# The last half of the output columns computed in PSUM behind the last gather, the final work on one engine, and an account with exact extents

## The chip, the cores and the metric

The kernel runs on one core of one Trainium2 chip. The metric is the device time of one execution in microseconds (us), measured from a launch on the chip; the profile's span, from the first to the last instruction, is somewhat shorter. TensorE (PE) multiplies into PSUM banks, VectorE (DVE), ScalarE (ACT) and GpSimd (POOL) work on SBUF (and DVE and ACT on PSUM), SyncE (SP) issues most of the DMAs, POOL some. Each engine works through its own instructions in program order.

## The reference

One layer of a streaming encoder, for 2048 tokens of 1024 channels behind 16 learned meta tokens, in float32:

```python
u = rms_norm(h, pre_g)
proj = u @ w_in                       # 7 x 512 columns
# glu_a, glu_b, conv_gate, q, k, v, sb_gate
c = causal_depthwise_conv(glu_a * sigmoid(glu_b), conv_w, conv_b)   # width 31
c = (silu(layer_norm(c)) @ w_pw2 + b_pw2) * silu(conv_gate)
s = stick_breaking_attention(heads(q), heads(k), heads(v))          # 8 heads x 64
s = s * silu(sb_gate)
mixed = concatenate([c, s], axis=-1) @ w_out
return h + rms_norm(mixed, post_g)
```

The attention is strictly causal: the weight of a key is sigmoid(z) times the product of 1 - sigmoid(z) over the keys between it and the query. Since the final normalisation needs the sum of squares over all 1024 output columns of a token, nothing of a token's output can leave before all its columns are there.

## The kernel before

The tokens are worked on in four chunks of 512 (TC). All large products are made at float32 accuracy from a rounded high part and the rest as a low part, three matmuls for one (hi x hi, hi x lo, lo x hi). A weight slab arrives raw (`wr<-wpack`, 512 KB, a ring of two), ACT rounds its high half (`w<-wr`), POOL takes the difference (`w<-wr,w`); both halves are saved in DRAM by POOL (`wscr<-w`) and read back in later chunks (`w<-wscr`, ring of four, at the end also `wr<-wscr`). `load_raw` issues the raw loads, `prepare` fills the rings, `weights` hands a slab to a product and `release` frees it. In `attention` each step is one product q x k (`T<-kk,q`), a sigmoid on ACT (`T<-T`), a scan on DVE (`pr<-T,pr`), four transposes on PE (`T<-ident,pr`), the high and low part of the result on ACT (`ah<-T`) and DVE (`al<-T,ah`), and the products with the values (`av<-ah,vk`, `av<-al,vk`), called gather. Eight heads of 64 channels go in four pairs; a pair's result, gated, becomes one of four `mixs` slabs of 128 rows, the convolution's result the four `mixc` slabs.

The order is made when the kernel is built, by a list scheduler: `merge` takes pieces of the attention as its main stream and pieces of projections and of the output product as filling between them, in shares that the table `SHARES` gives for each chunk. It chooses by an account, the `Clock`: every instruction that is issued adds an estimated time to its engine, and `Clock.at` tells when a tile will be ready. Work that isn't due yet waits as `Later` in the list `soon`, and `step`, `force` and `run` issue it. So a change of an estimate or of a rule moves instructions everywhere; what was issued first stands first in its engine's queue.

In the last chunk, `last_room` reuses two large tiles for what the end needs, `later_part` loads the last 128 rows of w_out early (`ev<-wpack` four times, split on ACT and POOL into `acc` tiles) and calls `out_part`. That makes the output product for the first seven of eight 128-row slabs (k below 7) of the mixer's result, in four column groups of 256 (OC); each group for two halves of 256 tokens. Three groups go by ACT into the SBUF tiles `y`; the last group stays in two `mm` banks, and the end of its second half (`keep["rest"]`) is made in `out_last`, when the heads are done. When the last head's gather has been made, `finish_late` computes the last `mixs` slab, and `out_last` works through four blocks of 128 tokens (`add_up`): the products of the last slab (`T<-acc,mixs`, `mm<-acc,mixs`), additions to `y` on DVE, squares summed on ACT, multiplication by post_g on POOL for the first 512 columns and on DVE for the rest, then `rate` (the reciprocal root by a power on POOL) and `give_out` (scaling, addition of x, and the DMA of the output; of the first two blocks the second half by ACT and POOL, all the rest by DVE).

## Time and profile before

| | before |
|---|---|
| median of 3 runs | 1373.24 us (1370.44 to 1373.45) |
| the profiled execution | 1371.76 us, span 1370.0 us |
| PE busy | 1312.5 us, 96% of the span |
| DVE busy | 1006.8 us, 73% |
| ACT busy | 732.0 us, 53% |
| POOL busy | 657.0 us, 48% |
| moved by DMA | 299.12 MB, mean 218 GB/s |
| mean granted TensorE clock | 0.992 |

The engines work side by side, so their shares don't add up. The profile names an instruction by its engine, its operation and the tiles out<-in; numbers behind a tile's name are left out. All instructions are recorded at one helper's line, so one goes by tiles and not by lines. Idle time of an engine is given with what ended it: "[4.83 <-DVE al]" says that the engine stood for 4.83 us until DVE had written `al`.

### The profile page before, as it was taken

To read this page: it belongs to the slowest core of one execution; us is meant where nothing else is said; L and a number is where in the kernel's file an instruction comes from. 1 tells how busy PE (TensorE), PEld (TensorE's weight loads), DVE (VectorE), ACT (ScalarE), POOL (GpSimd) and SP (SyncE) were. 2 spreads that over 40 slices of the span, in tenths; PEclk is the share of its full clock that TensorE was granted. 3 is DMA by queue.
4 is the path that set the end of the run, shared out by engine and by line. 5 is a ranking of instruction groups with operands and counts; after the bars stand their busy time and mean duration, and the time that the engine had idled before them with its cause. 6 is when DMAs were issued, how large, how long until landed. Compare 5 with 4: busy or idle time off the path is not lost. (4 is left out here: it accounts for less than half of the span.)

```text
span 1370.0 us, 21785 instructions
## 1 busy us (share of the span) xinstructions
PE 1312.5 (96%) x7599; PEld 1125.2 (82%) x7599; DVE 1006.8 (73%) x1402; ACT 732.0 (53%) x1452; POOL 657.0 (48%) x794
## 2 busy tenths in 40 slices
PE   6999988999998999999999999999999999999895
PEld 5998877887788977887789988888777898888794
DVE  3999663998984467984495477885549988898666
ACT  5233554444446544476655456578676576655443
POOL 5445486668356631387831243278786111222303
PEclk9999999999999999999999999999999999999998
DMA  4266978999975994686866696567677456587431
GB/s 142 94 164 197 345 233 248 302 316 320 348 245 179 319 339 145 202 236 204 264 223 185 191 326 198 173 190 235 201 220 241 147 173 174 173 276 237 159 109 62
DMA packets 160157, 299.12 MB, mean 218 GB/s; under 512 B 15392, under 2 KB 69344, under 8 KB 160048
## 3 DMA queue, kind: packets, MB, share of 16 engines
q1 hardware_dynamic: 145744, 247.65, 58.9%
q0 software_dynamic: 14304, 50.08, 9.4%
q8 instruction: 60, 0.98, 0.3%
q14 instruction: 49, 0.40, 0.1%
HBM read 216.02 MB, written 81.66 MB: 217 GB/s over the span
## 5 line engine op out<-in xcount | busy, mean ns | idle before, releaser
L204 PE MATMUL mm<-uh,w 128*128 128x512 f32 (+1 forms) x1728 | 522.9, 367 | 2.6 <-POOL w L204 1.5
L204 PEld LDWEIGHTS mm<-uh,w 128*128 128x128 f32 x1728 | 307.6, 188 | 51.5 <-POOL w L204 2.5
L204 DVE TENSOR_TENSOR al<-T,ah 128x512 fp32r<-128x512 f32 (+3 forms) x323 | 194.4, 602 | 168.9 <-ACT ah L204 167.9
L204 PE MATMUL mm<-ul,w 128*128 128x512 f32 (+1 forms) x864 | 312.0, 361 | 0.0
L204 DVE TENSOR_TENSOR_SCAN pr<-T,pr,zcol 128x512 f32<-128x512 f32 x192 | 245.1, 1277 | 55.5 <-ACT T L204 51.4
L204 ACT ACTIVATE ah<-T 128x512 fp32r<-128x512 f32 (+3 forms) x323 | 171.7, 532 | 164.7 <-PE T L204 159.5
L204 DVE SCALAR_TENSOR_TENSOR cv<-ct,cp,cv 128x512 f32<-128x512 f32 x319 | 239.4, 751 | 7.5
L204 ACT ACTIVATE T<-T 128x512 f32<-128x512 f32 (+2 forms) x320 | 167.6, 525 | 96.6 <-PE T L204 92.7
L204 POOL TENSOR_TENSOR acc<-acc,pd 128x512 f32<-128x512 f32 x150 | 193.8, 1292 | 50.6 <-ACT pd L204 43.7
L204 PE MATMUL T<-kk,q 128*128 128x512 f32 (+2 forms) x640 | 195.3, 388 | 2.9 <-DVE pr L204 1.7
L204 POOL TENSOR_TENSOR w<-wr,w 128x512 fp32r<-128x512 f32 x116 | 149.7, 1296 | 98.5 <-ACT w L204 95.2
L204 PE MATMUL T<-ident,pr 128*128 128x128 f32 x1088 | 173.2, 275 | 9.8 <-DVE al L204 6.5
L204 PEld LDWEIGHTS mm<-ul,w 128*128 128x128 f32 x864 | 162.7, 188 | 20.3 <-DVE ul L204 0.2
L204 PEld LDWEIGHTS T<-ident,pr 128*128 128x128 f32 x1088 | 134.1, 141 | 42.3 <-DVE al L204 8.2
L204 DVE TENSOR_TENSOR_SCAN pr<-T,tri 128x128 f32<-128x128 f32 (+3 forms) x128 | 103.8, 815 | 43.0 <-ACT T L204 42.5
L204 ACT ACTIVATE w<-wr 128x512 fp32r<-128x512 f32 x116 | 72.3, 628 | 104.8 <-DMA wr<-wpack 34.9
L204 PEld LDWEIGHTS T<-kk,q 128*128 128x128 f32 x640 | 106.1, 190 | 19.1 <-DVE pr L204 2.8
L204 PE MATMUL av<-ah,vk 128*128 128x512 f32 (+1 forms) x320 | 117.0, 366 | 1.4 <-ACT ev L204 1.4
L204 PE MATMUL av<-al,vk 128*128 128x512 f32 (+1 forms) x320 | 117.4, 367 | 0.0
L204 PE MATMUL mm<-uh,wr 128*128 128x512 f32 x320 | 115.0, 401 | 0.0
L204 ACT ACTIVATE pd<-ct,cp 128x512 f32<-128x512 f32 x150 | 105.9, 717 | 15.3 <-POOL acc L204 14.7
L204 POOL COPY cm<-pr 128x1 f32<-128x1 f32 x120 | 23.3, 206 | 153.4 <-DVE pr L204 153.2
(154 smaller groups left out, 1768.3 us busy)
## 6 DMA issues: line engine op xcount, KB each, us to landing
w<-wscr SPq DMA_DIRECT2D x125, 512.0 KB, 4.2
wscr<-w POOLq DMA_DIRECT2D x76, 512.0 KB, 5.8
wr<-wscr SPq DMA_DIRECT2D x59, 512.0 KB, 4.3
wr<-wpack SPq DMA_DIRECT2D x58, 512.0 KB, 5.2
kk<-kscr SPq DMA_DIRECT2D x80, 256.0 KB, 5.2
vk<-vscr SPq DMA_DIRECT2D x80, 256.0 KB, 4.1
q<-qscr SPq DMA_DIRECT2D x64, 256.0 KB, 6.8
tok<-x SPq DMA_DIRECT2D x16, 512.0 KB, 7.6
```

The costliest lines, as they stand in the source:

```text
L204: return call(out, *args, **kw)
```

## The change

*Tail.* `out_part` takes only the first two column groups into `y`. For the last two, `late(0, ...)` makes the product of k below 7 for tokens 0 to 255 in the banks `cv` and `mm` during the attention; `late(1, ...)` for tokens 256 to 511, in the banks `mm` and `T`, becomes `keep["rest"]`, so that it stands in `out_last`, with three steps ahead of the first final products and the others behind them. The weights of these groups are loaded a second time for it. In `out_last` DVE does all multiplications, additions and scalings; POOL keeps four powers and one memset; the addition of epsilon becomes a fourth column of the sums. `AHEAD` goes, and one corner of `SHARES` for the last chunk moves from 136.0 to 126.3.

*Account.* `Clock.at` looks at the parts of a tile that were written with their full extent instead of their offset; `Later` pieces get an order in which nested ones stand with their parent, and only earlier ones are forced by a later instruction. A new rule in `merge` (`early`) runs a waiting piece whose time has come before the next attention step; `load_raw` loads one raw slab at a time as such a piece; `room_for_turned` keeps transposes from being issued when the ring of `ah` has no free tile.

*Late split.* The split of the last 128 rows of w_out is put into `soon` with a date 6 and 7 us ahead.

```diff
-AHEAD = 2
-    [(29.8, 172.7)], [(73.1, 217.8)], [(116.0, 217.8)], [(125.1, 97.4), (160.4, 136.0)],
+    [(29.8, 172.7)], [(73.1, 217.8)], [(116.0, 217.8)], [(125.1, 97.4), (160.4, 126.3)],
...
         lo, hi = extent(ap)
-        hit = [t for o, t in parts.items() if lo <= o <= hi]
-        return max(hit or parts.values())
+        return max([0.0] + [t for (a, b), t in parts.items() if a <= hi and lo <= b])
...
-        self.n = Later.count
+        self.n = (*clock.here, Later.count)
...
             for a in (*ins, *outs):
-                for e in c.writers(a):
+                for e in c.writers(a, c.here):
                     self.run(e)
...
+            if c + 1 < NCH:
+                yield from proj_specs(c + 1)
+            else:
+                for n in (*range(0, D, OC), *range(D // 2, D, OC)):
+                    yield w_out, n, OC, 0, KD - 1
...
-    def load_raw():
-        while todo_raw and len(raws) < RAWS:
+    def load_raw(most=RAWS):
+        while todo_raw and len(raws) < most:
...
-                    in_us(2.0, load_raw)
+                    when(
+                        lambda: load_raw(min(RAWS, len(raws) + 1)), [], date=pe.now + 2.0, tag="wr")
...
-                    yield need(*f[0]["a"], tag="T")
+                    yield need(*f[0]["a"], tag="T", given=room_for_turned)
...
-        for n in range(0, D, OC):
+        for n in range(0, D // 2, OC):
...
+        def late(i, tags):
+            for e in range(2):
+                w = weights(w_out, D // 2 + e * OC, OC, 0, KD - 1)
+                keep["o", i, e] = yield from out_products(
+                    w, mix, range(KD - 1), i, False, tag=tags[e], free=True
+                )
+
+        yield from late(0, ("cv", "mm"))
+        keep["rest"] = late(1, ("mm", "T"))
...
+        def add_first(tb, a):
+            yt = y[tb // 2][:, tb % 2, 0:TC]
+            dve.tensor_tensor(yt, yt, a, op=ALU.add)
+            square(tb, yt, 0)
+            dve.tensor_tensor(yt, yt, pg[:, 0], op=ALU.mult)
+
+        def add_second(tb):
+            yt = y[tb // 2][:, tb % 2, TC:]
+            for e in range(2):
+                o, cols = keep["o", tb // 2, e][:, tb % 2], slice(e * OC, (e + 1) * OC)
+                square(tb, o, 1 + e)
+                dve.tensor_tensor(yt[:, cols], o, pg[:, 1, cols], op=ALU.mult)
...
-            dve.tensor_scalar(ss, ss, 1e-6, None, op0=ALU.add)
...
-                if h and tb < 2:
-                    act.activation(yt[:, cols], yt[:, cols], AF.Copy, scale=r)
-                    pool.tensor_tensor(xr, xr, yt[:, cols], op=ALU.add)
-                else:
-                    dve.scalar_tensor_tensor(xr, yt[:, cols], r, xr, op0=ALU.mult, op1=ALU.add)
+                dve.scalar_tensor_tensor(
+                    xr, y[tb // 2][:, tb % 2, cols], rates[tb], xr, op0=ALU.mult, op1=ALU.add
+                )
...
+        rest = keep["rest"]
+        for _ in range(3):
+            next(rest)
+        a = [first(0)]
+        second(0)
+        a += [first(tb) for tb in range(1, NTB)]
+        add_first(0, a[0])
+        finish_off(rest)
+        second(1)
+        add_second(0)
+        add_first(1, a[1])
+        rate(0)
+        add_second(1)
+        add_first(2, a[2])
+        rate(1)
+        give_out(0)
+        add_first(3, a[3])
+        give_out(1)
+        add_second(2)
+        rate(2)
+        add_second(3)
+        rate(3)
+        give_out(2)
+        give_out(3)
...
+            early = [e for e in soon if e.at() < s.at()] if s.at() > pe.now + LEAD else ()
+            if early:
+                run(min(early, key=lambda e: e.at()))
+                continue
             s.go()
...
-            split(raw, hi, lo)
+            in_us(
+                6.0 + i, lambda raw=raw, hi=hi, lo=lo: split(raw, hi, lo), [raw], [hi, lo]
+            )
```

The first place is the end of PE's queue, from the last gathers on (`av<-ah,vk` and `av<-al,vk`), before:

```order
L204 MATMUL av<-ah,vk 128x512
L204 MATMUL av<-al,vk 128x512
L204 MATMUL av<-ah,vk 128x512
L204 MATMUL av<-al,vk 128x512
L204 MATMUL mm<-w,mixs 128x256 x6
L204 MATMUL mm<-w,mixc 128x256 x24
L204 MATMUL mm<-w,mixs 128x256 x18
L204 MATMUL T<-acc,mixs 128x512 x3
L204 MATMUL T<-acc,mixs 128x256 x3
L204 MATMUL mm<-acc,mixs 128x256 x6
L204 MATMUL T<-acc,mixs 128x512 x3
L204 MATMUL T<-acc,mixs 128x256 x3
```

and of the change:

```order
L203 MATMUL av<-ah,vk 128x512
L203 MATMUL av<-al,vk 128x512
L203 MATMUL mm<-w,mixc 128x256 x12
L203 MATMUL mm<-w,mixs 128x256 x18
L203 MATMUL mm<-wr,mixc 128x256 x24
L203 MATMUL T<-acc,mixs 128x512 x3
L203 MATMUL cv<-acc,mixs 128x256 x6
L203 MATMUL mm<-acc,mixs 128x256 x6
L203 MATMUL T<-acc,mixs 128x512 x9
L203 MATMUL mm<-w,mixs 128x256 x18
L203 MATMUL T<-w,mixc 128x256 x24
L203 MATMUL T<-wr,mixs 128x256 x18
```

Behind the last gather stood 48 matmuls of 256 columns ahead of the first product of the last `mixs` slab (`T<-acc,mixs`); now there are 54, and 60 more (18, 24, 18) behind the final products of all four blocks' first half.

The second place is the end of DVE's queue, from the first addition of the third block on, before (`tok` are the tiles `y`, `uh` holds post_g, `ul` holds x):

```order
L204 TENSOR_TENSOR tok<-tok,T 128x512
L204 TENSOR_REDUCE ss<-sq_15301 128x1
L204 TENSOR_SCALAR ss<-ss 128x1
L204 TENSOR_TENSOR tok<-tok,T 128x256
L204 TENSOR_TENSOR tok<-mm,uh 128x256
L204 TENSOR_TENSOR tok<-tok,uh 128x256
L204 TENSOR_REDUCE ss<-sq_15331 128x1
L204 TENSOR_SCALAR ss<-ss 128x1
L204 SCALAR_TENSOR_TENSOR ul<-tok,st_15338,ul 128x512 x2
L204 SCALAR_TENSOR_TENSOR ul<-tok,st_15349,ul 128x512 x2
```

and of the change, from the first addition of the third block on:

```order
L203 TENSOR_TENSOR tok<-tok,T 128x512
L203 TENSOR_TENSOR tok<-tok,uh 128x512
L203 TENSOR_REDUCE ss<-sq_15155 128x1
L203 SCALAR_TENSOR_TENSOR ul<-tok,st_15302,ul 128x512 x2
L203 TENSOR_TENSOR tok<-tok,T 128x512
L203 TENSOR_TENSOR tok<-tok,uh 128x512
L203 SCALAR_TENSOR_TENSOR ul<-tok,st_15316,ul 128x512 x2
L203 TENSOR_TENSOR tok<-mm,uh 128x256
L203 TENSOR_TENSOR tok<-T,uh 128x256
L203 TENSOR_REDUCE ss<-sq_15155 128x1
L203 TENSOR_TENSOR tok<-mm,uh 128x256
L203 TENSOR_TENSOR tok<-T,uh 128x256
```

The four multiplications of 512 columns (`tok<-tok,uh`) are new on this engine, the additions of 256 columns and the addition of epsilon (`ss<-ss`) are gone, and the multiplications of 256 columns now read their product from a PSUM bank (`cv`, `mm`, `T`).

The third place is SP's queue between chunk 0 and chunk 1, where values for the next chunk's attention (`vm`, `vk`), gates (`gscr`) and raw weights (`wr`) are moved, before:

```order
L204 DMA q_1989<-qscr 64x2x512 x2
L204 DMA kk<-kscr 128x512
L204 DMA wr<-wpack 128x2x512
L204 DMA gscr<-ev 128x512
L204 DMA wr<-wpack 128x2x512
L204 DMA gscr<-ev 128x512
L204 DMA wr<-wpack 128x2x512
L204 DMA vm<-vscr 16x64 x16
L204 DMA vk<-vscr 128x4x128
L204 DMA q_2221<-qscr 64x2x512 x2
L204 DMA kk<-kscr 128x512
L204 DMA wr<-wpack 128x2x512 x4
```

and of the change:

```order
L203 DMA q_1988<-qscr 64x2x512 x2
L203 DMA kk<-kscr 128x512
L203 DMA gscr<-ev 128x512
L203 DMA wr<-wpack 128x2x512 x2
L203 DMA gscr<-ev 128x512
L203 DMA vm<-vscr 16x64 x16
L203 DMA vk<-vscr 128x4x128
L203 DMA wr<-wpack 128x2x512 x2
L203 DMA q_2270<-qscr 64x2x512 x2
L203 DMA kk<-kscr 128x512
L203 DMA wr<-wpack 128x2x512 x3
```

The write of `gscr` now stands ahead of the first of these raw loads, and the raw load that stood ahead of the 16 `vm` loads stands behind them and `vk`, with another one, ahead of `q`. On ACT, whose two roundings of a slab (`w<-wr`) stand near the normalised tokens of chunk 1 (`uh<-T,cp`), before:

```order
L204 ACTIVATE mixc<-mm 128x512
L204 ACTIVATE w<-wr 128x512 x2
L204 ACTIVATE T<-T 128x128
L204 ACTIVATE mixc<-mm 128x512
L204 ACTIVATE uh<-T,cp 128x512 x3
L204 ACTIVATE w<-wr 128x512 x2
L204 ACTIVATE ah<-T 128x128
L204 ACTIVATE T<-T 128x256
L204 ACTIVATE uh<-T,cp 128x512 x2
```

and of the change:

```order
L203 ACTIVATE mixc<-mm 128x512
L203 ACTIVATE w<-wr 128x512 x2
L203 ACTIVATE ah<-T 128x256
L203 ACTIVATE T<-T 128x128
L203 ACTIVATE mixc<-mm 128x512
L203 ACTIVATE w<-wr 128x512 x2
L203 ACTIVATE uh<-T,cp 128x512 x3
L203 ACTIVATE ah<-T 128x128
L203 ACTIVATE T<-T 128x256
L203 ACTIVATE uh<-T,cp 128x512 x2
```

The two roundings behind the first three `uh` stand ahead of them now.

## Rows read from the trace of the kernel before

**Rows 1.** The page: the span, and the busy time of each engine with its share of the span and its instructions.

```profile
span 1370.0 us, 21785 instructions
...
PE 1312.5 (96%) x7599; PEld 1125.2 (82%) x7599; DVE 1006.8 (73%) x1402; ACT 732.0 (53%) x1452; POOL 657.0 (48%) x794
```

**Rows 2.** Busy time of each engine in five stretches (columns: stretch in us and its length; busy us and instructions of PE, PEld, DVE, ACT and POOL; the granted TensorE clock; the share of DMA time; GB/s).

```profile
165.00:225.00 60.00, 51.12 (x250) 41.43 (x249) 30.78 (x40) 31.86 (x61) 38.24 (x48) 0.97 0.76 243
225.00:1265.00 1040.00, 1024.85 (x5711) 866.83 (x5709) 775.79 (x1053) 590.93 (x1168) 511.50 (x611) 1.00 0.73 234
...
1294.30:1328.00 33.70, 33.70 (x250) 31.66 (x249) 22.34 (x30) 15.41 (x30) 0.92 (x1) 1.00 0.43 129
1328.00:1342.10 14.10, 14.10 (x105) 13.07 (x105) 5.41 (x9) 4.79 (x8) 0.00 (x0) 1.00 0.15 49
...
1353.65:1370.00 16.35, 0.00 (x0) 0.00 (x0) 12.60 (x21) 3.99 (x14) 8.04 (x8) 0.61 0.34 128
```

**Rows 3.** Timeline of PE around the last attention product (columns: start, us, engine, line, operation, out<-in, shapes, count; in brackets the idle time before and what ended it). A line groups neighbours that follow each other.

```profile
1341.71 0.39 PE L204 MATMUL av<-al,vk 128*128 128x512 f32 x1
1341.93 0.88 PE L204 MATMUL mm<-w,mixs 128*128 128x256 f32 x6
...
1345.53 2.32 PE L204 MATMUL mm<-w,mixs 128*128 128x256 f32 x18
1347.68 1.21 PE L204 MATMUL T<-acc,mixs 128*128 128x512 f32 x6
```

**Rows 4.** Timeline of DVE over the tail, same columns.

```profile
1343.47 0.42 DVE L204 TENSOR_TENSOR uh<-uh 128x256 f32<-128x256 f32 x1
...
1348.58 1.02 DVE L204 TENSOR_TENSOR tok<-tok,T 128x512 f32<-128x512 f32 x2 [2.26 <-PE T L204]
...
1350.46 1.22 DVE L204 TENSOR_TENSOR tok<-tok,uh 128x256 f32<-128x256 f32 x1 [0.38 <-ACT ev L204]
...
1354.62 1.74 DVE L204 SCALAR_TENSOR_TENSOR ul<-tok,st,ul 128x512 f32<-128x512 f32 x1
...
1360.99 0.67 DVE L204 TENSOR_TENSOR tok<-tok,T 128x512 f32<-128x512 f32 x1
1361.59 0.14 DVE L204 TENSOR_REDUCE ss<-sq 128x1 f32<-128x3 f32 x1
...
1364.23 2.73 DVE L204 SCALAR_TENSOR_TENSOR ul<-tok,st,ul 128x512 f32<-128x512 f32 x4
```

**Rows 5.** Timeline of ACT over the tail: the squares of 512 and of 256 columns.

```profile
1349.30 0.63 ACT L204 ACTIVATE ev<-tok 128x512 bf16<-128x512 f32 x1 [3.44 <-DVE tok L204]
...
1350.33 0.36 ACT L204 ACTIVATE ev<-mm 128x256 bf16<-128x256 f32 x1
```

**Rows 6.** Timeline of POOL over the tail: one of its multiplications.

```profile
1353.15 1.26 POOL L204 TENSOR_TENSOR tok<-tok,uh 128x512 f32<-128x512 f32 x1
```

**Rows 7.** Timelines of ACT (two rows) and of PE (one row) at the start.

```profile
13.60 2.18 ACT L204 ACTIVATE w<-wr 128x512 fp32r<-128x512 f32 x4
15.68 1.83 ACT L204 ACTIVATE uh<-T,cp 128x512 fp32r<-128x512 f32 x3
...
17.19 2.41 PE L204 MATMUL T<-ident,tok 128*128 128x128 f32 x16 [0.99 <-DVE ul L204]
```

**Rows 8.** Timeline of SP (SPq is its queue) between chunk 0 and chunk 1: DMA issues, their time in the queue and their count.

```profile
176.45 0.39 SPq L204 DMA_DIRECT2D wr<-wpack  x1
176.94 0.52 SPq L204 DMA_DIRECT2D gscr<-ev  x1
...
191.76 0.38 SPq L204 DMA_DIRECT2D wr<-wpack  x1
192.20 9.88 SPq L204 DMA_DIRECT2D vm<-vscr  x16
...
205.06 10.91 SPq L204 DMA_DIRECT2D wr<-wpack  x3
```

**Rows 9.** Timelines of ACT (two rows) and of PE (three rows) between chunk 0 and chunk 1.

```profile
169.79 1.06 ACT L204 ACTIVATE ev<-tok 128x1024 bf16<-128x1024 f32 x1 [1.13 <-DMA gscr<-ev]
...
212.35 1.15 ACT L204 ACTIVATE w<-wr 128x512 fp32r<-128x512 f32 x2 [7.80 <-DMA wr<-wpack]
...
172.74 0.33 PE L204 MATMUL T<-ident,pr 128*128 128x128 f32 x1 [1.50 <-DVE pr L204]
174.01 0.47 PE L204 MATMUL mm<-uh,w 128*128 128x512 f32 x1 [0.95 <-DVE ev L204]
...
214.04 1.11 PE L204 MATMUL T<-ident,pr 128*128 128x128 f32 x4 [4.83 <-DVE al L204]
```

**Rows 10.** Busy time in the two stretches between 165 and 1290 us in which the granted clock was about half (columns as in rows 2).

```profile
213.60:217.05 3.45, 3.01 (x9) 2.57 (x10) 3.36 (x6) 3.04 (x7) 3.45 (x5) 0.51 0.12 15
1275.20:1282.00 6.80, 6.05 (x20) 4.73 (x20) 6.25 (x12) 1.93 (x6) 1.82 (x3) 0.50 0.26 78
```

**Rows 11.** Timelines of ACT (one row) and of PE (three rows) where the last raw weights arrive.

```profile
1271.34 0.63 ACT L204 ACTIVATE acc<-ev 128x512 fp32r<-128x512 f32 x1 [2.90 <-DMA ev<-wpack]
...
1273.24 0.66 PE L204 MATMUL T<-ident,pr 128*128 128x128 f32 x4 [1.26 <-DVE al L204]
1274.43 0.51 PE L204 MATMUL T<-kk,q 128*128 128x256 f32 x2 [0.53 <-DVE pr L204]
...
1276.25 1.65 PE L204 MATMUL T<-ehl,vm 128*128 128x512 f32 x3 [0.75 <-DVE al L204]
```

More of the change, by code (lines that the diff above doesn't have):

```diff
@@ L91, in __init__, with readers @@
         self.soon = []
+        self.here = ()
     def writers(self, ap, before=None):
         return [e for e in self.soon if e.touches(e.outs, ap) and (not before or e.n < before)]
-    def readers(self, ap):
-        return [e for e in self.soon if e.touches(e.ins, ap)]
+    def readers(self, ap, before=None):
+        return [e for e in self.soon if e.touches(e.ins, ap) and (not before or e.n < before)]
     def at(self, ap, before=None):
@@ L180, in issue @@
             for a in (*ins, *outs):
-                for e in c.writers(a):
+                for e in c.writers(a, c.here):
                     self.run(e)
             for a in outs:
-                for e in c.readers(a):
+                for e in c.readers(a, c.here):
                     self.run(e)
@@ L200, in issue @@
             for a in outs:
-                c.ready.setdefault(a.name, {})[a.offset] = done
+                c.ready.setdefault(a.name, {})[extent(a)] = done
             for a in (*outs, *near):
@@ L261, in run @@
             soon.remove(e)
+            here, clock.here = clock.here, e.n
             e.what()
+            clock.here = here
     def force(mark):
-        for e in clock.writers(mark):
-            run(e)
+        while clock.writers(mark):
+            run(clock.writers(mark)[0])
     def when(what, ins, outs=(), engine=None, date=0.0, tag=None):
@@ L393, in step, with tap @@
             tap_apart()
-    def tap():
-        if next(taps[0], None) is None:
-            taps.popleft()
+    def tap(some=taps):
+        here, clock.here = clock.here, ()
+        if next(some[0], None) is None:
+            some.popleft()
+        clock.here = here
     def tap_apart():
-        if next(taps_apart[0], None) is None:
-            taps_apart.popleft()
+        tap(taps_apart)
     def fill_gap(when):
@@ L477, in chunk @@
                 yield w_pw2, j * P, P, 0, NJ
-            yield from proj_specs(c + 1) if c + 1 < NCH else out_specs(0, KD - 1)
+            if c + 1 < NCH:
[3 more added lines that the diff above has]
+                    yield w_out, n, OC, 0, KD - 1
         for spec in proj_specs(0):
@@ L1018, in load_first, with room_for_turned @@
             keep["first", c] = load_q(c, 0), load_k(0, c)
+    def room_for_turned():
+        return clock.oldest("ah", 3) not in hold
     def attention(c, mixs):
@@ L1290, in meta_keys @@
             fetch(js[0])
-        yield need(bm, tag="T")
+        yield need(bm, tag="T", given=None if part else room_for_turned)
         hold.remove(bm.name)
@@ L1321, in meta_keys, with out_products @@
             mixs[j] = hi, lo
-    def out_products(w, mix, ks, half, whole=True, bank=None, there=None):
+        hold.remove(ah.name)
+    def out_products(w, mix, ks, half, whole=True, bank=None, there=None, tag="mm", free=None):
         fresh = bank is None
@@ L1333, in out_products @@
                 nxt = [m for kk in pair for m in mix(kk)]
-                yield need(wh, wl, *nxt, tag=None if bank is not None else "mm")
+                yield need(wh, wl, *nxt, tag=None if bank is not None else tag)
             if bank is None:
-                bank = PT("mm", [P, 2, OC])
+                bank = PT(tag, [P, 2, OC])
             for b in range(2):
@@ L1345, in out_products @@
                 pe.matmul(o, ml, wh, start=False, stop=(whole and i == len(ks) - 1 and b == 1))
-            if half and (k % 2 or i == len(ks) - 1):
+            if (half if free is None else free) and (k % 2 or i == len(ks) - 1):
                 release()
@@ L1355, in out_part @@
         there = lambda k: k < NJ or k - NJ in mixs[c]
-        for n in range(0, D, OC):
-            last = n == D - OC
+        for n in range(0, D // 2, OC):
             w = weights(w_out, n, OC, 0, KD - 1)
@@ L1367, in out_part @@
             for i in range(2):
-                part = out_products(w, mix, ks, i, not last, banks[i], there)
-                if last and i == 1:
-                    first = next(part)
-                    for _ in range(AHEAD):
-                        yield first
-                        first = next(part)
-                    keep["rest"] = part
-                    return
-                b = yield from part
-                if last:
-                    keep["o", 0] = b
-                else:
-                    act.activation(y[i][:, :, n : n + OC], b, AF.Copy)
+                b = yield from out_products(w, mix, ks, i, True, banks[i], there)
+                act.activation(y[i][:, :, n : n + OC], b, AF.Copy)
+        def late(i, tags):
[6 more added lines that the diff above has]
+        keep["rest"] = late(1, ("mm", "T"))
     def out_last(y, mh, ml):
@@ L1391, in out_last, with first, second @@
         pg = keep["pg"]
-        edge = TC + OC
         w0, w1 = keep["w", 0], keep["w", 1]
-        sums, rates = {}, {}
-        def products_of(tb):
-            i, b = divmod(tb, 2)
-            a, b1 = PT("T", [P, TC]), PT("T", [P, OC])
+        sums, rates = T("sq2", [P, NTB, 4], 1), {}
+        pool.memset(sums[:, :, 3:], 1e-6)
+        def first(tb):
+            a = PT("T", [P, TC])
             products(a, tb, *w0, True, True)
-            products(b1, tb, *(t[:, 0:OC] for t in w1), True, True)
-            if b == 0:
-                for e in range(2):
-                    products(
-                        keep["o", i][:, e], 2 * i + e, *(t[:, OC:] for t in w1), False, e == 1
-                    )
-            return a, b1, keep["o", i][:, b]
+            return a
+        def second(i):
+            for e in range(2):
+                for b in range(2):
+                    w = (t[:, e * OC : (e + 1) * OC] for t in w1)
+                    products(keep["o", i, e][:, b], 2 * i + b, *w, False, b == 1)
         def square(tb, src, n):
```

35 lines of the change are left out of this document (6 added, 29 removed).

## The prediction, written before the changed kernel ran

> **What bounds it now.** I read the page's busy shares first, then windows by stage, then the timeline at each stage's edge. TensorE (PE) is busy 1312.5 of 1370.0 us [rows 1]: before the tail only PE's gaps and its clock can be won. The windows say where they are: 225 to 1265 us PE is busy 1024.85 of 1040.00 us, in 165 to 225 us only 51.12 of 60.00, and in the last 16.35 us not at all, while VectorE (DVE) works 12.60 of them [rows 2]. So three places can pay: the tail, the joint of chunk 0 and chunk 1, and the start.
>
> The tail is a chain. The last attention product starts at 1341.71 us (call this L). Behind it PE has 48 matmuls of 256 columns, starting at 1341.93, and the first product of the last mixer rows at 1347.68; so one such matmul costs 5.75/48 = 0.12 us [rows 3]. DVE's first addition follows 0.90 us behind that product, at 1348.58 [rows 4]. From there DVE, ScalarE (ACT) and POOL pass each 128-token block on, and the span ends at 1370.0, L + 28.29.
>
> **The change, part by part.**
>
> *Matmuls behind the last gather.* The second half of the columns, k below 7, for tokens 256 to 511 is left until the heads are done. The order shows 54 + 60 = 114 matmuls of 256 columns behind the last gather where 48 stood (the 12 between the last two gathers are left out). PE's work in all is the same, so what stands ahead of L shrinks by 66 x 0.12 = 7.9 us, as long as PE is the bound there: it is busy 33.70 of 33.70 us from 1294.30 to 1328.00 and 14.10 of 14.10 to 1342.10 [rows 2]. Term: **-7.9**. But DVE, which does the scans and differences of the same steps, is busy 22.34 of that 33.70; in 25.8 us it would be at 87%, and single steps must wait on it. Bounds: nothing, to half of the gain. I take **+1.0**, near nothing since DVE's total still fits.
>
> *From L to the end.* Ahead of the first final product stand 54 matmuls and the last gather: 0.22 + 6.5 = 6.7; DVE begins 0.90 later, L + 7.6 (before: L + 6.87). DVE then has all the work. A 512-wide addition repeats after 0.60 (1360.99 to 1361.59), a 256-wide operation with nothing beside it took 0.42 (1343.47), a reduction 0.14, an output operation 2.73/4 = 0.68 [rows 4]. I cost a 512-wide multiply as an addition. Eight at 0.60, eight at 0.42, four at 0.14, eight at 0.68: 14.2. Each of four blocks waits for ACT's square between addition and multiply, 0.63 [rows 5] and some 0.25 of handing over: 3.5. That is L + 25.3; from the last DVE operation to the end before are 1370.0 - 1366.96 = 3.04 [rows 4]: L + 28.3. PE has its last result about 6.7 + 12 x 0.12 + 9 x 0.24 + 72 x 0.12 = L + 18.9, and DVE reaches it only at about L + 20.6, so the moved matmuls are covered; without that cover each microsecond of them would come on top.
>
> The POOL multiplies go. Beside a POOL multiply of 1.26 us [rows 6] DVE's 256-wide multiply took 1.22 us, a 512-wide output operation 1.74; alone 0.42 and 0.68 [rows 4]. So moving POOL's work to DVE costs DVE less than it looks: what DVE gains by undisturbed operations (4 x 0.8 + 2 x 1.06 = 5.3 us) nearly pays four multiplies at 0.60 and two output operations at 0.68 (3.8 us). The Trainium skill, page "SBUF — State Buffer", section "Who interferes with whom", says that a VectorE instruction with two SBUF inputs contends with a GpSimd instruction that reads SBUF; the trace agrees in these rows.
>
> One thing speaks against the change. Squares (ACT) and multiplies (DVE) now read the same PSUM bank, and the order makes each wait for the other: DVE's multiply of a bank behind ACT's square, and for the second block of a pair ACT's square behind DVE's multiply of the first. A square of 256 takes 0.36 [rows 5]. Only in the last pair nothing stands before it; bounds nothing and two squares with handing over, 1.2; I take 0.3. The Trainium skill, "PSUM — Partial Sum Buffer", section "PSUM bank collisions raise a hardware error", says that two engines must not touch one bank at once, reads included, so the compiler orders them; by it the two reads are strictly one behind the other, and the sum takes the upper bound, 0.9 us more than mine. Tail behind L: 28.6 against 28.29, **+0.3**.
>
> *Second loading of the weights.* Eight more 512 KB loads in the last stage, where the DMA share is 0.43 and then 0.15 [rows 2]; they hide, as their rings come free while others are used. Late, they would stop PE ahead of the tail.
>
> *Start.* The account moves four weight roundings on ACT ahead of `uh`. Before, they held ACT from 13.60 to 15.68 between two `uh`, and PE waited 0.99 us at 17.19 [rows 7]. Raw weights are there early. **-0.9** (bounds 0 and -1.0).
>
> *Chunk 0 to 1.* On SP a raw load stood at 176.45 ahead of a `gscr` write (176.94), and ACT's 1.13 us ahead of 169.79 were a wait for such a write [rows 9]: a raw load holds SP until POOL frees a raw tile. Then a load sent at 191.76 stood ahead of 16 `vm` loads (9.88 us), and the next raws went at 205.06 [rows 8]; ACT waited 7.80 us for them at 212.35, PE 4.83 us at 214.04, and 1.50 and 0.95 at 172.74 and 174.01 [rows 9]. From 213.60 to 217.05 the granted clock was 0.51 [rows 10], that is the 1.2 GHz level after a gap, 3.45 x 0.49 = 1.7 us. In all 9.0. Changed, `gscr` goes first, the `vm` loads no longer stand behind the second raw, and two raws follow `vk` ahead of `q`: one at about the old 191.8, the next some 9 us sooner than 205. ACT's roundings then come ahead of `uh`. Bounds 0 and -9.0; something else is usually late next (POOL's low halves), so half: **-4.5**. `gscr` ahead can be worth 2.5 of the 9.0 by itself.
>
> *Late split and exact extents.* At 1271.34 ACT waited 2.90 us for the last raw slab (`acc<-ev`), PE then lost 1.26, 0.53 and 0.75 us [rows 11], and the clock was 0.50 for 6.80 us [rows 10], 3.4 us: 5.9 in all. The order puts the split only one rounding later, and the same loads stand in front; I take **0**, bounds -5.9 and +2.9 (the wait once more). Elsewhere in 225 to 1265 us 15.15 us of idle PE time are all that can be won [rows 2], and moved steps may lose as much as they win: 0, bounds -4 and +4.
>
> Sum: -7.9 + 1.0 + 0.3 - 0.9 - 4.5 = -12.0. The profiled execution took 1371.76 us; the median of the three runs, 1373.24, is 1.48 above. 1373.24 - 12.0 = **1361**.
>
> **The rivals.** A change under 0.2% (2.7 us) can hardly be told from none here.
>
> *The tail alone pays*: the joint is stopped by something else (POOL waits: it is also busy there, 38.24 of 60.00 [rows 2]). 1373.24 - 6.6 = 1366.6. For it: in a tight account one late piece follows another. Against it: the late load, ACT's wait for it and PE's gap stand one behind another in the rows [rows 8, 9]. 0.22.
>
> *The joint is recovered in full*: -7.9 + 1.0 + 0.3 - 0.9 - 9.0 = -16.5, 1357. For it: PE has enough to do there otherwise. 0.16.
>
> *The steps ahead of L become latency-bound*: DVE, at 87%, waits for ACT between a scan and a difference, which gives back some 5 of the 7.9 us, and the order brings nothing: 1373.24 - 2.9 + 0.3 = 1370.6. Against it: ACT and DVE have gaps now because PE is full. 0.09, half of it within 0.2%.
>
> *Slower*: with less fill, gaps of about 1 us come between the attention steps and PE falls to the 1.2 GHz level, as after 1.26 + 0.53 + 0.75 us of gaps at 1273 to 1276 [rows 10, 11]. The stretch 1294.30 to 1328.00 keeps 25.8 us of PE work, which then takes twice as long. It decides from 12.0 us of work at the low level; the whole stretch gives 1361 + 25.8 = 1387. Against it: there is still fill between the steps, and the drop needed several gaps. 0.07.
>
> *The change doesn't do what it says*: the second half isn't behind the heads. The order excludes it.
>
> **How the numbers follow.** The likeliest, 0.41, is 1361, its own range 1358 to 1365. The remaining 0.05 are steps moved at other places that lose more than is won, between same and slower. Faster: 0.41 + 0.22 + 0.16 + 0.04 = 0.83; same 0.07; slower 0.10. The range takes in the full joint with a part of the 1265 us bounds below it and the latency-bound case above: 1353 to 1371.
>
> **What would show it.** In the changed trace: last gather about 12 us earlier by the span, and about 28.6 us from there to the end; DVE without multiplies of over 1 us and PE's last matmul about L + 19. At the joint: `gscr` not behind a raw load, no PE gap of 4.8 us, clock 1.00 at 214; PE's first full stretch from about 18.4 instead of 19.36. Wrong is the tail's term if PE has gaps between the last attention steps, or if DVE waits on ACT's squares for more than 5 us in all; wrong is the joint's term if ACT waits there for a raw that went later than now.

## The result and the profile after

| | before | changed |
|---|---|---|
| median | 1371.62 us (1370.44 to 1373.45, 5 runs) | 1358.79 us (1354.69 to 1362.14, 5 runs) |
| ratio to before | | 0.9902, 95% interval 0.9877 to 0.9927 |
| the profiled execution | 1371.76 us, span 1370.0 us | 1356.25 us, span 1354.5 us |

The forecast was 1361 us, 12.0 us less than before; the medians differ by 12.8 us. The profiled executions differ by 15.5 us, since the runs of the changed kernel lie further apart (7.5 us) and its profiled one was its second shortest. The total is right. The parts are not, as the rest of this document shows: the tail brought nearly twice its share (11.7 us instead of 6.6), and the account less than half (2.3 instead of 5.4). That the two errors cancel is luck.

The page of the changed kernel, its span and busy times (as [rows 1]):

```profile
span 1354.5 us, 21801 instructions
...
PE 1311.8 (97%) x7599; PEld 1126.6 (83%) x7599; DVE 1006.0 (74%) x1400; ACT 732.5 (54%) x1448; POOL 649.4 (48%) x789
```

PE, DVE and ACT work as long as before, within 1 us, POOL 7.6 us less; the gain is PE's idle time. Windows of the changed kernel (columns as in [rows 2]), the start, the joint of chunk 0 and 1, the place of the last raw weights, the last attention steps and the tail:

```profile
0.00:30.00 30.00, 15.24 (x94) 13.93 (x95) 14.38 (x15) 17.01 (x29) 14.20 (x33) 1.00 0.43 145
...
165.00:225.00 60.00, 55.77 (x268) 45.12 (x267) 38.31 (x49) 36.36 (x67) 41.52 (x53) 0.97 0.84 288
...
1265.00:1290.00 25.00, 22.02 (x141) 18.20 (x140) 20.43 (x31) 11.36 (x22) 10.09 (x11) 1.00 0.54 178
1290.00:1316.00 26.00, 26.00 (x186) 23.80 (x186) 20.69 (x30) 14.71 (x29) 0.43 (x2) 1.00 0.43 137
1316.00:1336.00 20.00, 20.00 (x155) 19.13 (x154) 7.06 (x15) 5.15 (x12) 0.00 (x0) 1.00 0.74 224
```

and two stretches of the kernel before that were not among [rows 2]:

```profile
0.00:30.00 30.00, 17.91 (x124) 15.93 (x125) 10.22 (x16) 17.26 (x29) 15.71 (x34) 1.00 0.46 149
...
1265.00:1290.00 25.00, 20.99 (x120) 17.50 (x119) 20.45 (x35) 12.11 (x24) 10.94 (x11) 0.86 0.52 164
```

The start has become worse: PE is busy 15.24 of the first 30 us where it was 17.91. In the joint it works 55.77 of 60.00 us (before 51.12). Between 1265 and 1290 us the granted clock stays at 1.00 (before 0.86). From 1290 to 1336 us PE has no gap at all, with less filling than before.

So that whole executions can be compared, I worked out the time that PE lost in each stage, from windows like these: idle time plus busy time times (1 - granted clock). The limits are the same in all four kernels, but for the last gather's start. Each column is one execution: that of the kernel before took as long as its median (1371.76 against 1371.62), the others 2.5, 1.6 and 2.5 us less than theirs. So the columns say where time was lost, and the medians what a change is worth.

| lost PE time, us | before | changed | tail alone | account alone |
|---|---|---|---|---|
| 0 to 30 | 12.1 | 14.8 | 12.1 | 14.8 |
| 30 to 165 | 1.0 | 1.1 | 1.0 | 1.0 |
| 165 to 232 (joint) | 10.6 | 6.1 | 9.7 | 6.4 |
| 232 to 410 | 1.9 | 0.7 | 1.5 | 0.7 |
| 410 to 442 | 5.2 | 6.0 | 4.2 | 4.9 |
| 442 to 1255 | 8.1 | 6.2 | 8.4 | 6.5 |
| 1255 to 1295 | 7.2 | 3.0 | 2.2 | 5.2 |
| 1295 to the last gather | 0.0 | 0.0 | 0.0 | 0.1 |
| sum | 46.1 | 37.9 | 39.1 | 39.6 |

The last gather starts at 1327.03 instead of 1341.71 us, 14.7 sooner: 8.2 of it are lost time saved, the other 6.5 work that now stands behind it. From there to the end of the span are 27.5 us, before 28.3. The timeline of PE around the last gather in the changed kernel (as [rows 3]):

```profile
1327.03 0.40 PE L203 MATMUL av<-al,vk 128*128 128x512 f32 x1
1327.26 1.58 PE L203 MATMUL mm<-w,mixc 128*128 128x256 f32 x12
...
1345.57 0.87 PE L203 MATMUL T<-acc,mixs 128*128 128x256 f32 x6
```

and of DVE over the tail (as [rows 4]):

```profile
1335.95 0.69 DVE L203 TENSOR_TENSOR tok<-tok,uh 128x512 f32<-128x512 f32 x1 [0.79 <-ACT ev L203]
...
1347.02 0.41 DVE L203 TENSOR_TENSOR tok<-mm,uh 128x256 f32<-128x256 f32 x1
1347.36 0.41 DVE L203 TENSOR_TENSOR tok<-T,uh 128x256 f32<-128x256 f32 x1
1347.69 0.14 DVE L203 TENSOR_REDUCE ss<-sq 128x1 f32<-128x4 f32 x1
1347.98 0.42 DVE L203 TENSOR_TENSOR tok<-mm,uh 128x256 f32<-128x256 f32 x1
...
1348.75 2.73 DVE L203 SCALAR_TENSOR_TENSOR ul<-tok,st,ul 128x512 f32<-128x512 f32 x4
```

PE has its last product at 1345.57 + 0.87 = 1346.44, 19.4 us behind the gather (before 11.9), and VectorE begins with the second half of the last pair of blocks 0.58 us later, at 1347.02. The multiplications of 512 columns take 0.69 us and none of VectorE's operations is stretched any more.

### The profile page after: what moved, and what is told of

Same layout as the page of the kernel before. It is cut to its first block, busy times and chain, and to the rows that moved or that the text cites. A ratio compares the mean times of both kernels' runs of the same rounds, so it can differ in the third digit from the quotient of the medians.

```text
span 1354.5 us, 21801 instructions
## 1 busy us (share of the span) xinstructions
PE 1311.8 (97%) x7599; PEld 1126.6 (83%) x7599; DVE 1006.0 (74%) x1400; ACT 732.5 (54%) x1448; POOL 649.4 (48%) x789
## 4 chain that ended last, share of the span: by engine, by line
PE 76%; DVE 8%; DMA 6%; ACT 3%; issue 3%; POOL 2%; SPq 0%; DVEq 0%; ACTq 0%; POOLq 0%
PE mm L203 50%; PE T L203 18%; PE av L203 8%; DMA tok<-x 2%; DVE pr L203 2%; ACT ev L203 1%; DVE cv L203 1%; DVE tok L203 1%; DVE al L203 1%; DVE acc L203 1%; DMA q<-qscr 1%; POOL ev L203 1%; DMA ev<-x 1%; DMA wscr<-w 1%; DVE ul L203 1%
```

## Experiments

The short names in the table are those of the sections below. The experiments came in three groups, each with its own runs of the kernel before, so the ratios are to be compared and not the medians.

| kernel | median, us | ratio to before, interval |
|---|---|---|
| changed | 1358.79 | 0.9902 (0.9877 to 0.9927) |
| changed, once more | 1358.82 | 0.9904 (0.9887 to 0.9920) |
| tail alone | 1359.17 | 0.9915 (0.9898 to 0.9933) |
| account alone | 1368.30 | 0.9983 (0.9971 to 0.9996) |
| meta tokens on ACT | 1355.78 | 0.9893 (0.9874 to 0.9912) |
| scaling on ACT | 1352.99 | 0.9863 (0.9846 to 0.9880) |
| first roundings held back | 1354.92 | 0.9875 (0.9855 to 0.9895) |
| POOL multiplies | 1358.39 | 0.9901 (0.9884 to 0.9917) |
| old corner of SHARES | 1360.74 | 0.9919 (0.9902 to 0.9936) |
| three findings together | 1349.68 | 0.9837 (0.9819 to 0.9855) |
| old raw loads | 1363.51 | 0.9941 (0.9922 to 0.9960) |

### Tail alone

The parts of the diff from `out_specs` on (two more column groups in the list of weights, `out_products` with a tag, `out_part`, `out_last`) and the corner of `SHARES`, put into the kernel before. The first 6974 of PE's 7599 matmuls stand in the order of the kernel before, up to about 1257 us.

```diff
-        for n in range(0, D, OC):
+        for n in range(0, D // 2, OC):
...
+        yield from late(0, ("cv", "mm"))
+        keep["rest"] = late(1, ("mm", "T"))
...
# Clock, Later, load_raw, merge, later_part: as before
```

> The kernel before with the tail of the change alone: the halved out_part, late, the new out_last, the second loading of the weights and the corner of SHARES; the account, the raw loads and the split of the last weights as before. Theory (the parts add up): the last gather comes 8 us sooner than before, about 27.5 us stand behind it as in the changed kernel, the gaps at the start and between chunk 0 and 1 stay as they were: about 1371.6 - 8.7 = 1363, and a joint with its 4.8 us gap. Rival (the shorter stretch ahead of the last gather only works with the new rules of the account): gaps between the last attention steps or a clock at half there, 1367 or more.

Measured: 0.9915, that is 11.7 us less than before, 3 us more than the theory said. The rival is out: there is no gap from 1295 us to the last gather. Timelines of PE, ACT and PE:

```profile
213.80 0.66 PE L202 MATMUL T<-ident,pr 128*128 128x128 f32 x4 [4.48 <-DVE al L202]
...
1269.71 0.63 ACT L202 ACTIVATE acc<-ev 128x512 fp32r<-128x512 f32 x1 [0.73 <-DMA ev<-wpack]
...
1269.98 1.69 PE L202 MATMUL mm<-w,mixc 128*128 128x256 f32 x12
```

The joint's gap is still there (4.48 us at 213.80). But at 1269.71 ACT has waited 0.73 us only for the last raw weights, and behind the transposes at 1269.57 PE has filling to do, 12 products `mm<-w,mixc`. In the kernel before PE stood 1.26, 0.53 and 0.75 us there and then ran at half clock [rows 10, 11]. This stage lost 2.2 us instead of 7.2 (table above): these 5 us were not forecast, and they come with the tail. So the main parts are 6.4 us of work moved behind the last gather, 0.8 less from there to the end, and these 5. The profiled execution won 2.0 more ahead of 1255 us, where PE's order is that of the kernel before; that is difference between executions.

### Account alone

The reverse: the changed kernel with the tail and `SHARES` of before. Its first 6974 matmuls on PE stand in the order of the changed kernel, up to about 1253 us.

```diff
+        for n in range(0, D, OC):
-        for n in range(0, D // 2, OC):
...
# Clock, Later, load_raw, merge, room_for_turned, later_part: as in the change
```

> The changed kernel with the tail, the weights of the end and SHARES of before: only the account, the raw loads and the late split are changed. Theory: what was won between 165 and 1290 us stays (9 us less idle time), what was lost at the start too (2.7 us), and the tail is that of before: about 1371.6 - 6 = 1365.5. Rival (the gain lies in the tail alone, and the rest is noise between runs): 1371.

Measured: 0.9983, 2.3 us less than before, between theory and rival. With the 11.7 us of the tail that makes 14.0, and the change brought 13.4 (0.9902 of 1371.6): the parts add up. The profiled execution was one of its shortest, 6.0 us below that of the kernel before; in which stage its longer executions lose the other 3.7, no profile shows. The joint lost 6.4 us, nearly as in the changed kernel. But behind 1255 us the stall is back, though the split is held back. Timelines of ACT and PE:

```profile
1267.63 0.63 ACT L205 ACTIVATE acc<-ev 128x512 fp32r<-128x512 f32 x1 [4.08 <-DMA ev<-wpack]
...
1269.53 1.04 PE L205 MATMUL T<-ident,pr 128*128 128x128 f32 x4 [2.42 <-DVE al L205]
```

ACT waits 4.08 us for the raw weights, PE 2.42 us behind it. The stage lost 5.2 us instead of 7.2, but nearly all of these 2.0 are the clock (0.96 instead of 0.91); PE's idle time there is 3.8 us instead of 4.0.

### The corner of SHARES

```diff
-    [(125.1, 97.4), (160.4, 126.3)],
+    [(125.1, 97.4), (160.4, 136.0)],
```

> The changed kernel with the corner of SHARES for the last chunk at 136.0 as before; the order differs from the last 170 us on only. The tail alone won some 5 us between 1265 and 1290 us that were not forecast, where the wait for the last raw weights no longer stops PE. Theory A (the corner moved filling of 12 matmuls between the steps there): with the old corner the gap of 1 to 2.5 us and the half clock are back, 1362 to 1364. Theory B (the second half, left for later, is what fills): no gap, and the time within 1 us of 1358.8.

Measured: 0.9919; the intervals overlap, so the time alone doesn't tell. Timelines of ACT and of PE, and of ACT in the changed kernel:

```profile
1269.21 0.63 ACT L203 ACTIVATE acc<-ev 128x512 fp32r<-128x512 f32 x1 [3.42 <-DMA ev<-wpack]
...
1271.11 0.66 PE L203 MATMUL T<-ident,pr 128*128 128x128 f32 x4 [1.76 <-DVE al L203]
...
1268.11 0.63 ACT L203 ACTIVATE acc<-ev 128x512 fp32r<-128x512 f32 x1 [2.10 <-DMA ev<-wpack]
```

ACT waits 3.42 us and PE 1.76: theory A, for the gap. In the changed kernel ACT waits too, 2.10 us, but PE's gaps next to it are 0.28, 0.59 and 0.21 us. That stage lost 5.0 us against 3.0. So the corner puts filling between these steps, and a held back split does not replace it. The corner is worth 2.0 of the 4.2 us that the change won here; what the other 2.2 go by is not taken apart.

### The start: what made VectorE late

In the changed kernel five rows show why PE got its first projection 4 us later (POOL, DVE twice, PE twice); the last two are of DVE and POOL in the kernel before:

```profile
13.03 4.93 POOL L203 TENSOR_TENSOR w<-wr,w 128x512 fp32r<-128x512 f32 x4
...
13.08 5.42 DVE L203 TENSOR_SCALAR q<-q,st 16x1024 f32<-16x1024 f32 x1 [0.70 <-POOL st L203]
18.43 2.71 DVE L203 SCALAR_TENSOR_TENSOR ul<-T,cp,uh 128x512 fp32r<-128x512 f32 x4
...
19.22 1.03 PE L203 MATMUL T<-ident,q 16*128 16x16 f32 x8 [3.75 <-DVE ul L203]
...
23.41 0.37 PE L203 MATMUL mm<-uh,w 128*128 128x264 f32 x1
...
13.14 0.74 DVE L204 TENSOR_SCALAR q<-q,st 16x1024 f32<-16x1024 f32 x1 [0.70 <-POOL st L204]
...
14.29 4.97 POOL L204 TENSOR_TENSOR w<-wr,w 128x512 fp32r<-128x512 f32 x4 [1.18 <-ACT w L204]
```

The scaling of the 16 meta tokens took 5.42 us on VectorE, 13.08 to 18.50, while POOL made four differences of weights back to back (13.03 to 17.96). Before, it took 0.74 us from 13.14 on, and POOL began at 14.29 only. Two kernels take the two apart in different ways. First, the scaling goes to ScalarE:

```diff
-        dve.tensor_scalar(m, m, r[:NM], None, op0=ALU.mult)
+        act.activation(m, m, AF.Copy, scale=r[:NM])
```

> The changed kernel with one instruction moved: the scaling of the meta tokens (q<-q,st, 16x1024) on ScalarE instead of VectorE. Theory (that VectorE operation took 5.42 us instead of 0.74 because POOL's four differences of the first weights ran back to back beside it): the 5.42 us are gone, PE's gap of 3.75 us behind the first transposes shrinks to about 1, and the time falls by some 3 us, 1355.5 to 1356.5. Rival (VectorE's input was late, POOL has nothing to do with it): ScalarE's scaling ends as late, about 18 us, and the time stays at 1358.8.

Measured: 0.9893. Timelines of ACT and PE:

```profile
13.33 1.15 ACT L203 ACTIVATE q<-q,st 16x1024 f32<-16x1024 f32 x1 [1.36 <-POOL st L203]
...
17.97 3.68 PE L203 MATMUL T<-ident,tok 128*128 128x128 f32 x16 [2.14 <-DVE ul L203]
```

The scaling took 1.15 us from 13.33 on, so its input was not late, and PE's gap is 2.14 instead of 3.75 us. That speaks for the theory, but not alone: ACT, which does the scaling ahead of the four roundings, gets to these at 14.39 only, and POOL's differences begin at 15.08 instead of 13.03. The gain in time is within the interval. Second, nothing moves but the first four roundings on ScalarE:

```diff
+    late_w = [4]
...
-        when(high, [y], [hi, lo])
+        late_w[0] -= 1
+        when(high, [y], [hi, lo], date=13.0 if late_w[0] >= 0 else 0.0)
```

> The changed kernel with the first four roundings of weights (w<-wr) held back on ScalarE until the first four uh, as in the kernel before they stood behind the first; nothing else moves on any engine. Theory (POOL's differences beside it, not the data, made VectorE's scaling of the meta tokens 5.42 us long): with POOL starting some 3 us later the scaling takes 0.74 us again, PE's gap of 3.75 us goes, the first projection starts at about 19.4 instead of 23.41 us, and the time is 1358.8 - 4 = 1355. Rival (the scaling is long by itself in this order): 5.4 us again, and with the weights later 1359 to 1361.

Measured: 0.9875. Timelines of DVE, POOL and PE:

```profile
12.42 0.74 DVE L203 TENSOR_SCALAR q<-q,st 16x1024 f32<-16x1024 f32 x1 [0.70 <-POOL st L203]
...
16.13 5.06 POOL L203 TENSOR_TENSOR w<-wr,w 128x512 fp32r<-128x512 f32 x4 [3.75 <-ACT w L203]
...
17.87 0.39 PE L203 MATMUL mm<-uh,w 128*128 128x264 f32 x1 [0.40 <-ACT uh L203]
```

The same VectorE operation, in the same place of its queue, took 0.74 us, with POOL starting at 16.13; PE's order is that of the changed kernel throughout. The first projection starts at 17.87 instead of 23.41 us. Pooled over both measurements of the changed kernel (0.9903) the gain is 3.8 us, plus or minus about 3.3.

### The same cause at the joint

Rows of the changed kernel between chunk 0 and 1 (SP, DVE, POOL, PE; columns as in all timelines), and one of DVE in the kernel before:

```profile
176.94 0.33 SPq L203 DMA_DIRECT2D gscr<-ev  x1
...
186.35 9.04 SPq L203 DMA_DIRECT2D vm<-vscr  x16
...
195.96 3.19 SPq L203 DMA_DIRECT2D wr<-wpack  x2
...
181.81 3.52 DVE L203 TENSOR_SCALAR tok<-tok,st 128x1024 f32<-128x1024 f32 x1
185.25 0.68 DVE L203 TENSOR_TENSOR ev<-mm,ev 128x512 f32<-128x512 f32 x1
...
182.14 1.31 POOL L203 TENSOR_TENSOR w<-wr,w 128x512 fp32r<-128x512 f32 x1
...
185.99 0.50 PE L203 MATMUL mm<-uh,w 128*128 128x512 f32 x1 [2.41 <-DVE ev L203]
...
180.53 2.76 DVE L204 TENSOR_SCALAR tok<-tok,st 128x1024 f32<-128x1024 f32 x1
```

The `gscr` write goes ahead, the raw loads behind the `vm` loads at 195.96, as the order said. What PE waits for now is VectorE's `ev` (185.25), which stands behind a scaling of 3.52 us, where one with POOL idle took 0.74 (at 167.84); POOL again works through. The change did not make this from nothing: in the kernel before the scaling of the same tokens took 2.76 us, and the next one 1.73 where it is 3.81 now. Two additions ahead of it on VectorE took 3.01 us as well (from 176.84), where one alone took 0.67. The scaling of chunks 1 to 3 on ScalarE, beside that of the meta tokens:

```diff
-            dve.tensor_scalar(t, t, r, None, op0=ALU.mult)
+            if c:
+                act.activation(t, t, AF.Copy, scale=r)
+            else:
+                dve.tensor_scalar(t, t, r, None, op0=ALU.mult)
```

> As the kernel with the meta tokens scaled on ScalarE, and the scaling of the tokens of chunks 1 to 3 (tok<-tok,st, 128x1024) on ScalarE too. Theory (between chunk 0 and 1 these VectorE operations took 3.52 and 3.81 us beside POOL for the same reason): the 2.41 us gap at 186 us and the half clock behind it go, 4 us more: about 1352. Rival (ScalarE in order becomes late there itself, about 1.1 us for each of twelve): no gain over the kernel with the meta tokens alone, or a loss of some us.

Measured: 0.9863, by the ratios about 4 us less than with the meta tokens alone (2.8 by the medians), as the theory had it; the intervals overlap a little. Timelines of ACT, one of the twelve, and of PE:

```profile
177.71 1.13 ACT L203 ACTIVATE tok<-tok,st 128x1024 f32<-128x1024 f32 x1
...
176.76 0.80 PE L203 MATMUL T<-kk,q 128*128 128x256 f32 x2 [2.74 <-DVE al L203]
```

ScalarE takes 1.13 us. The 2.41 us gap is gone, but another of 2.74 us has come at 176.76. The joint lost 5.0 us of PE time, 6.1 in the changed kernel, but 5.0 too in a second execution of that kernel (below); the 10.0 with the meta tokens alone are of its slowest execution, with a gap of 3.29 us at 213.37. So the rows show that the scaling made the one gap; it is not shown that the gain of some 4 us comes from there.

### Raw loads as before

```diff
-                    when(
-                        lambda: load_raw(min(RAWS, len(raws) + 1)), [], date=pe.now + 2.0, tag="wr")
+                    in_us(2.0, load_raw)
```

> The changed kernel with one rule of the account undone: raw weights are loaded as before, as many as the ring holds (in_us(2.0, load_raw)). The order of SP and ScalarE between chunk 0 and 1 is then nearly that of the kernel before: a raw load ahead of gscr, one ahead of the 16 vm loads, and the roundings behind the first uh. Theory (the raw loads' place makes the gap there): PE's gap of 4 to 5 us at 214 us is back with the half clock, 1358.8 + 4 = 1363. Rival (the gap goes by the other rules, or comes back in any case): 1359.

Measured: 0.9941, some 5 us slower than the change, the size that the theory gave. But the gap is not the old one. Timelines of SP and PE:

```profile
194.51 0.38 SPq L203 DMA_DIRECT2D wr<-wpack  x1
194.95 9.55 SPq L203 DMA_DIRECT2D vm<-vscr  x16
...
194.38 0.80 PE L203 MATMUL T<-kk,q 128*128 128x256 f32 x2 [3.08 <-DVE pr L203]
```

The raw load stands ahead of the `vm` loads again and goes at 194.51. PE's gap is 3.08 us at 194.38, not 4.8 at 214, and the larger part is lost later: the joint lost 8.2 us instead of 6.1, and 4.8 went between 232 and 325 us, where the changed kernel loses nothing. So the raw loads' place is what the account gains with; that it was the gap at 214 us alone is not shown.

### The tail: POOL or VectorE

```diff
-            dve.tensor_tensor(yt, yt, pg[:, 0], op=ALU.mult)
+            pool.tensor_tensor(yt, yt, pg[:, 0], op=ALU.mult)
```

> The changed kernel with the four multiplications of 512 columns in the tail on POOL again, as before; nothing else differs. Theory (on POOL they take 1.27 us and stretch VectorE's operations with two SBUF inputs beside them to 1.7 us): from the last gather to the end 28.5 to 29.5 us instead of 27.47, 1360. Rival (VectorE saves four times 0.69 and 0.8 of waiting, POOL was the better place): 26 us, 1357.

Measured: 0.9901, no difference, and 27.1 us behind the last gather against 27.5: neither. Timelines of POOL and DVE:

```profile
1343.60 1.29 POOL L203 TENSOR_TENSOR tok<-tok,uh 128x512 f32<-128x512 f32 x1
...
1343.67 2.43 DVE L203 SCALAR_TENSOR_TENSOR ul<-tok,st,ul 128x512 f32<-128x512 f32 x2 [1.11 <-POOL st L203]
1346.49 0.42 DVE L203 TENSOR_TENSOR tok<-mm,uh 128x256 f32<-128x256 f32 x1 [0.39 <-ACT ev L203]
```

Beside POOL's multiplication two output operations take 2.43 us instead of 1.41, and POOL's third multiplication took 1.84 instead of 1.29 beside the two before, so they do slow one another. But VectorE gets to the last pair at 1346.49, and PE's last products end at 1346.59 in this kernel: what stands ahead of them is covered whichever engine does it.

### Three findings together

The roundings held back, the scaling of chunks 1 to 3 on ScalarE, and in the tail the next block's addition ahead of a block's multiplication (the first of these places):

```diff
-        add_second(0)
-        add_first(1, a[1])
+        add_only(1, a[1])
+        mult_first(0)
+        add_second(0)
```

> The changed kernel with three of the findings together: first roundings held back, scaling of chunks 1 to 3 on ScalarE, and in the tail the next block's addition between a block's addition and its multiplication, so that VectorE does not wait for the square. If the parts add up: 1353 (scaling on ScalarE, the start included at 21.0) - 1.5 (start at 19.4) - 0.6 (tail; TensorE's last products then end it) = 1351. Rival (what is won at the start is lost at the joint, where another wait ends last): 1353.

Measured: 1349.68 us, 0.9837, faster than both kernels; the parts add up. Timeline of DVE in the tail:

```profile
1329.69 0.69 DVE L203 TENSOR_TENSOR tok<-tok,T 128x512 f32<-128x512 f32 x1 [1.44 <-PE T L203]
1330.30 0.68 DVE L203 TENSOR_TENSOR tok<-tok,uh 128x512 f32<-128x512 f32 x1
...
1339.43 0.42 DVE L203 TENSOR_TENSOR tok<-mm,uh 128x256 f32<-128x256 f32 x1
1340.14 0.42 DVE L203 TENSOR_TENSOR tok<-T,uh 128x256 f32<-128x256 f32 x1 [0.29 <-ACT ev L203]
```

VectorE no longer waits for the square ahead of a multiplication of 512 columns (0.79 to 0.85 us, four times, in the changed kernel), yet from the last gather to the end there are 27.1 us, 0.4 less: PE's last products end at 1339.53, and the multiplication at 1340.14 waits for ACT's square of the last one. Between the profiled executions, nearly all of the gain comes from the start and the joint (10.6 and 3.7 us lost, against 14.8 and 6.1).

### The changed kernel once more

> The changed kernel itself, once more beside the others on one chip, for the spread of its own runs (1354.69 to 1362.14 before): the median again 1358 to 1360. If the spread comes from the joint of chunk 0 and 1, this profile shows another gap there than the 2.41 us at 186.

Measured: 0.9904. Its profiled execution has the same 2.41 us gap at the joint, another of 1.56 us at 210.63, and a clock of 1.00 there. That gap stands behind two waits of ACT for DMAs, 2.27 us at 201.31 (`wr<-wpack`) and 1.77 at 207.29 (`wscr<-w`), that the first execution does not have. So waits for DMAs, and whether the clock falls behind a gap, differ between executions of one order. But the two lie only 1.2 us apart, and both are among the shortest of this kernel: what makes the spread of 7 us is not shown.

## Why the prediction was right, and where it was not

**Work behind the last gather, -7.9 + 1.0: right in sum.** 6.5 us were found (1296.0 us of PE work at full clock ahead of the last gather before, 1289.5 after). PE had no gap from 1295 us on, so the term of 1.0 for VectorE at 87% was not a loss there, and it made good that the moved work came to less than 66 x 0.12. Why it did is left open. The rivals that the last steps become latency-bound, or that the clock falls there, did not happen.

**From the last gather to the end, +0.3: the size was off by 1.1 (-0.8 was measured), the reason partly wrong.** 27.5 us were found, 28.6 forecast. The waits for squares were 3.3 us in all (3.5 forecast), and the ordering of the two readers of a bank cost 0.15 us (0.3 were put in): VectorE's last two blocks go at 1347.02, 1347.36, 1347.98, and the time from 1347.69 + 0.14 to 1347.98 is that wait. VectorE's own operations were costed right. The step that failed is that PE's last products are well covered: they end at 19.4, not 18.9, and VectorE is there at 20.0, not 20.6; the two are nearly level, so that work taken from VectorE ahead of that point wins 0.4 us at most (the experiments with POOL and with the exchanged additions). The 18.9 leave out the first three products of 512 columns behind the 54 matmuls, 3 x 0.24 = 0.7. And the 5.3 us that VectorE saves beside POOL do not "nearly pay" the 3.8 of its new work, they are more.

**Start, -0.9: wrong.** It cost 2.7 us. The step took the position of the roundings on ScalarE for the only thing that changes, and did not ask what they set free: POOL's differences then start 1.3 us sooner and stand beside a VectorE scaling that lies on the path.

**Joint, -4.5: right in size, one reason missed.** 4.5 us less were lost; as the term was half of 9.0 because something else is usually late next, the close fit is in part luck. The raw loads' place is worth about that (the experiment with the old raw loads), the gap at 214 us is gone. What is late next is not POOL's low halves but VectorE's scaling beside them, which took 2.76 us in the kernel before already. The clock is 1.00 at 214, but in the first execution it falls from 186 us on instead. And of the 2.5 us that `gscr` ahead could be worth by itself, gaps of 0.79 and 0.94 us are left at 175.79 and 177.06.

**Late split and exact extents, 0: the step failed as a place.** The changed kernel lost 2.3 us less between 232 and 1255 us, within the bounds of 4. Between 1255 and 1295 us 4.2 us were won, within the bounds too, and the tail with its corner of SHARES, which puts products between the waits, wins them alone (5.0); the late split did not shorten the waits there, and the 2.0 us less in the kernel with the account alone are mostly the clock's. The prediction looked for the effect of the tail behind 1294 us only.

So the sum of 12.0 held by luck: the tail brought 11.7 us instead of 6.6, since it also fills the stage of the last raw weights, and the rest 2.3 instead of 5.4. Of that shortfall the traces show the start, which lost 2.7 where 0.9 were to be won; the profiled execution with the account alone makes it good elsewhere, the longer ones do not. The rival "the tail alone pays" was nearer in how the gain is shared out, but not in its reason, for the joint was not stopped by something else; and its time was over 7 us too long.

## What to carry to other kernels

An instruction that is moved ahead on one engine sets the next engine free sooner; ask what will then run beside that one, and whether the trace shows that the two slow one another. When products are put off to the end of a kernel, look at the stages where they become filling, not only at the end. And before work is taken off an engine in a tail, see whether another engine's last result comes at the same moment.

## What the runs showed of the hardware

A VectorE scaling from SBUF to SBUF beside POOL waited until POOL paused, not until POOL's instruction ended: 5.42 us beside four POOL operations that follow one another (13.03 to 17.96), 3.52 us beside POOL's work up to 184.77, 0.74 us alone (at 167.84, with POOL idle from 167.68 on). The Trainium skill, page "SBUF — State Buffer", section "Who interferes with whom", names `tensor_scalar` among the operations that can take the port shared with GpSimd, and says that whoever issues first gets it for the whole instruction; the trace agrees that VectorE was shut out, but the wait went on over several instructions of POOL, and the scaling at 181.81 was recorded 0.33 us ahead of POOL's first operation (POOL was issuing a DMA then) and still had to wait for it. At the start POOL itself was not slowed (4.93 us for four, 4.97 in the kernel before).

The granted clock fell behind a gap in one execution and not behind the same gap in another of the same kernel: behind 2.41 us of idle time it was 0.64 from 186 to 190 us, a mean of the two levels (1.2 and 2.4 GHz), in the first execution of the changed kernel, and 1.00 in the second. The window of the first:

```profile
186.00:190.00 4.00, 4.00 (x14) 3.23 (x15) 1.84 (x4) 1.17 (x3) 3.97 (x5) 0.64 0.74 289
```

That is 4.00 x 0.36 = 1.4 us between two runs of one kernel.
